# Gated sigmoid over a 256 MB matrix: loads and stores moved from two hardware DMA queues to one software queue, with the one-packet option

## Chip, cores, metric

One core of a Trainium2 chip. The metric is the device time of one execution in microseconds (us); smaller is better. Runs of the kernel before on a single core agree within about 0.2%.

## The reference

```python
def setup_inputs():
    return {"x": np.random.randn(8192, 8192).astype(np.float32)}

def reference(x):
    a, b = np.split(x, 2, axis=-1)
    return a * (1 / (1 + np.exp(-b)))
```

268.4 MB are read and 134.2 MB written: 402.65 MB go through the DMA engines, and per element there are one sigmoid and one multiplication.

## The kernel before

32 tiles of 256 rows. A partition holds two whole rows (64 KB) of x and two rows (32 KB) of the result; there are two slots of each, 192 KB per partition in all. Loads are issued by SyncE, stores by ScalarE, each on its own hardware queue. ScalarE takes the sigmoid in place, VectorE multiplies into the output slot.

```python
R = 2; SLOTS = 2
xs = [pool.tile([P, R * n_cols], fp32, name=f"x_sb{k}") for k in range(SLOTS)]
os = [pool.tile([P, R * half], fp32, name=f"o_sb{k}") for k in range(SLOTS)]
for i in range(n_tiles):
    # ... cut: which slot, which earlier instructions are known to be over
    load = nc.sync.dma_start(out=xs[i % SLOTS], in_=x_t[i])
    # ... cut: the first and last tile are computed in four parts, the others in one
    for k, (r, c) in enumerate(parts):
        b = rows[:, r, 1, c]
        sig = nc.scalar.activation(out=b, in_=b, func=SIG)
        mul = nc.vector.tensor_mul(out=packed[:, r, c], in0=rows[:, r, 0, c], in1=b)
        # ... cut: waits declared as implied; odd sigmoids wait for the old store
    # ... cut: the stores (nc.scalar.dma_start); the last tile's in four pieces
```

Of the kernel before, what the change touches and what calls it, by code (L numbers as in the profile page):

```python
# [1 line left out]

# [4 lines left out]


def _tiles(ctx, tc, x, out):









    nc = tc.nc
    P = nc.NUM_PARTITIONS  # L20
    DEP = mybir.DependencyInfo(mybir.DependencyClass.Sync, mybir.DependencyReason.DATA)
    fp32 = mybir.dt.float32
    SIG = mybir.ActivationFunctionType.Sigmoid

    n_rows, n_cols = x.shape
    half = n_cols // 2
    R = 2
    SLOTS = 2
    n_tiles = n_rows // (P * R)
    x_t = x.rearrange("(n p r) m -> n p (r m)", p=P, r=R)  # L30
    out_t = out.rearrange("(n p r) m -> n p (r m)", p=P, r=R)

    pool = ctx.enter_context(tc.tile_pool(name="io", bufs=1))
    xs = [pool.tile([P, R * n_cols], fp32, name=f"x_sb{k}") for k in range(SLOTS)]
    os = [pool.tile([P, R * half], fp32, name=f"o_sb{k}") for k in range(SLOTS)]

    def implied(later, *earlier):
        for e in earlier:
            tc.declare_no_dep(later.ins, e.ins, reason="follows from the waits that are kept")

    gone = [{k: [] for k in ("loads", "sigs", "muls", "stores")} for _ in range(SLOTS)]
    last_stores = [[] for _ in range(SLOTS)]
    for i in range(n_tiles):
        old = gone[i % SLOTS]
        freed = last_stores[i % SLOTS]
        now = {k: [] for k in old}
        rows = xs[i % SLOTS].rearrange("p (r h m) -> p r h m", r=R, h=2)
        packed = os[i % SLOTS].rearrange("p (r m) -> p r m", r=R)

        load = nc.sync.dma_start(out=xs[i % SLOTS], in_=x_t[i])  # L50
        implied(load, *old["loads"], *old["sigs"])
        now["loads"].append(load)

        if 0 < i < n_tiles - 1:
            parts = [(slice(0, R), slice(0, half))]
        else:
            w = half // 2
            parts = [
                (slice(r, r + 1), slice(c * w, (c + 1) * w)) for r in range(R) for c in range(2)
            ]  # L60
        def store(cols):
            ins = nc.scalar.dma_start(out=out_t[i, :, cols], in_=os[i % SLOTS][:, cols])  # L62
            now["stores"].append(ins)

        chunks = []
# [3 lines that stand above are left out]
            mul = nc.vector.tensor_mul(out=packed[:, r, c], in0=rows[:, r, 0, c], in1=b)  # L69
            implied(sig, *old["sigs"], *old["muls"], *old["loads"])  # L70
            implied(mul, *old["muls"], *old["loads"], *now["loads"])
            by_sigmoid = i % 2 == 1 and len(parts) == 1
            implied(mul, *(s for s in old["stores"] if by_sigmoid or s not in freed))
            if by_sigmoid:
                for s in freed:
                    tc.add_manual_dep(sig.ins, s.ins.name, DEP, reason="frees the output slot")
            tc.keep_in_program_order(sig)
            now["sigs"].append(sig)
            now["muls"].append(mul)
            chunks.append(slice(r.start * half + c.start, r.start * half + c.stop))  # L80
            if i == n_tiles - 1 and k > 0:
                store(chunks[k - 1])
        store(chunks[-1] if i == n_tiles - 1 else slice(0, R * half))
        for s in now["stores"]:
            implied(s, *old["loads"], *old["sigs"], *old["muls"], *now["loads"], *now["sigs"])
        for k in old:
            old[k] += now[k]
        last_stores[i % SLOTS] = now["stores"]


def _launch_early(nc):



    SP = mybir.EngineType.SP
    entry, body = (b.instructions for b in nc.main_func.blocks[:2])
    load = next(i for i in body if i.engine == SP and i.opcode == "DMACopy")
    assert not load.sync_info.on_wait
    body.remove(load)
    where = next(k for k, i in enumerate(entry) if i.engine == SP and i.opcode == "Drain")  # L100
    entry.insert(where, load)


def _close_on_sync(nc):





    SP, POOL = mybir.EngineType.SP, mybir.EngineType.Pool  # L110
    ACT = mybir.EngineType.Activation
    block = nc.main_func.blocks[2].instructions
    waits = block[0]
    assert waits.engine == SP and waits.opcode == "Drain" and len(waits.sync_info.on_wait) > 1
    pool = [i for i in block if i.engine == POOL]
    drain1, gather1, release1, reset, clear, drain2, gather2, release2 = pool
    assert reset.is_reset_sema and clear.opcode == "ISA"
    others = [i for i in block[1:] if i.engine != POOL]
    arrive = [i for i in others[: len(others) // 2] if i.opcode == "Drain"]
    assert len(arrive) == 4  # L120
    body = nc.main_func.blocks[1].instructions
    last = [i for i in body if i.engine == ACT and i.opcode == "DMACopy"][-1].sync_info.on_update[0].id
    final = [w for w in waits.sync_info.on_wait if w.id == last]
    assert len(final) == 1

    def event(engine, wait, update=()):
        return mybir.InstEventSemaphore(
            name=nc.get_next_instruction_name(),
            engine=engine,
            debug=waits.debug,  # L130
            sync_info=mybir.SyncInfo(on_wait=[wait], on_update=list(update)),
        )

    n = len(block)
    for lo, hi in ((reset.reset_range_start, last), (last + 1, reset.reset_range_stop)):
        if lo < hi:
            nc.gpsimd.sem_clear(range(lo, hi))
    clears = block[n:]
    assert clears and all(i.opcode == "ISA" for i in clears)
    back = mybir.SyncUpdate(  # L140
        sync_type="semaphore",
        id=last,
        ant_name=final[0].ant_name,
        update_mode="sem-sub-imm",
        update_value=final[0].wait_value,
        update_reg=None,
    )
    block[:] = [
        *arrive,
        drain1,  # L150
        gather1,
        *(event(POOL, w) for w in waits.sync_info.on_wait if w.id != last),
        reset,
        *clears,
        drain2,
        event(SP, final[0], [back]),
    ]


@with_exitstack  # L160
def kernel(
    ctx: ExitStack,
    tc: tile.TileContext,
    x: bass.AP,
    out: bass.AP,
):
    nc = tc.nc
    with ExitStack() as pools:
        _tiles(pools, tc, x, out)
    tc.close()  # L170
    tc.compile()
    _launch_early(nc)
    _close_on_sync(nc)


# [1 line left out]
_INS = ['x']  # L177
_OUTS = [((8192, 4096), 'float32')]


# [23 lines left out]
```

## Time and profile before

| | before |
|---|---|
| time, median | 933.24 us (933.08 to 933.77, 4 runs) |
| profiled span | 931.7 us |
| VectorE, ScalarE, GpSimd busy | 30%, 24%, 0% |
| DMA engines busy, rate | 9 or 10 tenths in all 40 slices, 432 GB/s |
| a load descriptor (64 KB), a store descriptor (32 KB), on one engine | 2.418 us, 1.213 us |
| one tile on one engine | 29.00 us |

The prediction below shows the page's main lines. Two more pieces are needed for the comparison. The first is the chain of waits of the kernel before in order of time (start, length, what): each piece "DMA" is a load from its issue to its landing, the sigmoid behind it starts when the load has landed, 0.02 to 0.09 us after the last engine's semaphore update.

```profile
60.58 42.21 DMA x_sb<-in_x_dram
...
102.88 7.04 ACT x_sb L68
...
118.66 42.09 DMA x_sb<-in_x_dram
...
160.84 7.04 ACT x_sb L68
...
218.77 7.04 ACT x_sb L68
...
856.90 7.04 ACT x_sb L68
```

The chain walks over every second tile. 102.88, 160.84, 218.77: steps of 57.9 to 58.0 us, two tiles of 29.00. From 102.88 to 856.90 are 754.0 us, 13 steps of 58.00. Nothing is lost from one end to the other.

The second is how the 16 DMA engines run together. A transfer is split over all 16 DMA engines, and each engine posts a short semaphore record (9 ns, 4 bytes) after its share. The time from the first engine's record to the last engine's record of the same transfer I call the **spread**. In the kernel before it is 0.57 us for load 0, 0.61 us for load 10 and 0.65 us for load 31: the engines stay together. A load has landed when the last engine is through. Loads and stores share an engine record by record: of 8238 pairs of successive records on one engine (60 to 890 us of the span, assigned to engines by their times) 8236 go from one queue to the other.

### The profile page before, as it was taken

What the parts mean: (1) busy time and instruction counts of PE and PEld (TensorE: products, weight loads), DVE (VectorE), ACT (ScalarE), POOL (GpSimd) and SP (SyncE); (2) the same over time, 40 slices, a digit from 0 to 9 for tenths busy, and PEclk for the clock granted to TensorE, in tenths of its full rate; (3) what the DMA queues carried; (4) which work ended last, traced back from release to release, by engine and by line L of the source; (5) the groups of instructions that cost most, each with busy time, mean ns of one, the idle gap of its engine ahead of it and who ended that gap; (6) DMA issues with size and microseconds to landing.
All of it is one profiled execution on the core that took longest, in us unless ns stands there. A gap on an engine that the chain in (4) does not pass through costs nothing.

```text
span 931.7 us, 247 instructions
## 1 busy us (share of the span) xinstructions
DVE 278.7 (30%) x38; ACT 227.1 (24%) x39; POOL 0.2 (0%) x4
## 2 busy tenths in 40 slices
DVE  0333213333133331233312333123331233312333
ACT  1323330233311333113331133311333113332033
POOL 0000000000000000000000000000000000000000
DMA  9999999999999999999999999999999999999999
GB/s 405 428 450 428 422 456 405 450 428 428 450 418 438 428 436 442 428 428 450 447 408 428 442 459 428 413 460 411 450 428 425 453 408 447 428 428 450 425 430 405
DMA packets 9649, 402.67 MB, mean 432 GB/s; under 512 B 1072, under 2 KB 1072, under 8 KB 1072
## 3 DMA queue, kind: packets, MB, share of 16 engines
q1 hardware_dynamic: 4608, 268.44, 66.6%
q10 hardware_dynamic: 5040, 134.22, 33.4%
q14 instruction: 1, 0.01, 0.0%
HBM read 268.44 MB, written 134.22 MB: 432 GB/s over the span
## 4 chain that ended last, share of the span: by engine, by line
DMA 73%; DVE 15%; ACT 12%; issue 0%; ACTq 0%
DMA x_sb<-in_x_dram 73%; DVE o_sb L69 15%; ACT x_sb L68 12%; ACTq L62 0%; ACTq L68 0%
## 5 line engine op out<-in xcount | busy, mean ns | idle before, releaser
L69 DVE TENSOR_TENSOR o_sb<-x_sb 128x8192 f32<-128x8192 f32 (+1 forms) x38 | 278.7, 7344 | 647.1 <-ACT x_sb L68 647.1
L68 ACT ACTIVATE x_sb<-x_sb 128x8192 f32<-128x8192 f32 (+1 forms) x38 | 225.8, 5952 | 695.6 <-DMA x_sb<-in_x_dram 694.4
L68 ACT ACT_TABLE_LOAD x1 | 1.3, 1283 | 0.8 <-PEq L188 0.8
L188 POOL MEMSET const-bfloat16-1.0<- 128x1 bf16 x1 | 0.1, 102 | 0.0
L188 POOL MEMSET const-uint8-127<- 128x1 uint8 x1 | 0.1, 102 | 0.0
L188 POOL MEMSET const-float32-0.0<- 128x1 f32 x1 | 0.1, 99 | 0.2 <-issue 0.2
L188 POOL MEMSET const-float32-1.0<- 128x1 f32 x1 | 0.1, 99 | 0.0
## 6 DMA issues: line engine op xcount, KB each, us to landing
out_dram<-o_sb ACTq DMA_DIRECT2D x31, 4096.0 KB, 34.7
out_dram<-o_sb ACTq DMA_DIRECT2D x4, 1024.0 KB, 5.6
x_sb<-in_x_dram SPq DMA_DIRECT2D x32, 42.2
```

Of the source, the lines that this page charges most:

```text
L68: sig = nc.scalar.activation(out=b, in_=b, func=SIG)
L69: mul = nc.vector.tensor_mul(out=packed[:, r, c], in0=rows[:, r, 0, c], in1=b)
L188: nc = _bacc.Bacc("TRN2", target_bir_lowering=False, num_devices=1)
```

## The change

The intent: one queue in which the transfers come in the order in which they are needed, so that a load does not share the engines with a store; fewer waits; and, with the option `single_packet=True`, less time per descriptor. From tile 2 on, store i and load i+2 are issued by GpSimd, right behind each other. Loads 0 and 1 and the four stores of the last tile stay on the hardware queues.

```diff
+    def in_one_packet(out, in_):
+        return nc.gpsimd.dma_start(out=out, in_=in_, single_packet=True)
...
+    def load(i, queue):
+        old = gone[i % SLOTS]
+        ins = queue(out=xs[i % SLOTS], in_=x_t[i])
+        implied(ins, *old["loads"], *old["sigs"])
+        loads.append(ins)
+
+    for i in range(SLOTS):
+        load(i, nc.sync.dma_start)
...
-        load = nc.sync.dma_start(out=xs[i % SLOTS], in_=x_t[i])
-        implied(load, *old["loads"], *old["sigs"])
-        now["loads"].append(load)
...
-            by_sigmoid = i % 2 == 1 and len(parts) == 1
-            implied(mul, *(s for s in old["stores"] if by_sigmoid or s not in freed))
-            if by_sigmoid:
-                for s in freed:
-                    tc.add_manual_dep(sig.ins, s.ins.name, DEP, reason="frees the output slot")
+            implied(mul, *(s for s in old["stores"] if s not in freed))
...
-        store(chunks[-1] if i == n_tiles - 1 else slice(0, R * half))
+        if i == n_tiles - 1:
+            store(chunks[-1], nc.scalar.dma_start)
+        else:
+            store(slice(0, R * half), in_one_packet)
...
+        if i + SLOTS < n_tiles:
+            load(i + SLOTS, in_one_packet)
```

More of the change, by code (lines that the diff above doesn't have):

```diff
@@ L39, in implied @@
             tc.declare_no_dep(later.ins, e.ins, reason="follows from the waits that are kept")
+    def in_one_packet(out, in_):
+        return nc.gpsimd.dma_start(out=out, in_=in_, single_packet=True)
     gone = [{k: [] for k in ("loads", "sigs", "muls", "stores")} for _ in range(SLOTS)]
     last_stores = [[] for _ in range(SLOTS)]
+    loads = []
+    def load(i, queue):
[5 more added lines that the diff above has]
+        load(i, nc.sync.dma_start)
     for i in range(n_tiles):
@@ L46, in _tiles @@
         now = {k: [] for k in old}
+        now["loads"].append(loads[i])
         rows = xs[i % SLOTS].rearrange("p (r h m) -> p r h m", r=R, h=2)
         packed = os[i % SLOTS].rearrange("p (r m) -> p r m", r=R)
-        load = nc.sync.dma_start(out=xs[i % SLOTS], in_=x_t[i])
-        implied(load, *old["loads"], *old["sigs"])
-        now["loads"].append(load)
         if 0 < i < n_tiles - 1:
@@ L60, in _tiles, with store @@
             ]
-        def store(cols):
-            ins = nc.scalar.dma_start(out=out_t[i, :, cols], in_=os[i % SLOTS][:, cols])
+        def store(cols, queue):
+            ins = queue(out=out_t[i, :, cols], in_=os[i % SLOTS][:, cols])
             now["stores"].append(ins)
@@ L81, in _tiles @@
             if i == n_tiles - 1 and k > 0:
-                store(chunks[k - 1])
-        store(chunks[-1] if i == n_tiles - 1 else slice(0, R * half))
+                store(chunks[k - 1], nc.scalar.dma_start)
+        if i == n_tiles - 1:
+            store(chunks[-1], nc.scalar.dma_start)
+        else:
+            store(slice(0, R * half), in_one_packet)
         for s in now["stores"]:
```

## The prediction

> **What bounds the kernel now.** I read the page first: busy shares of the compute engines, then the row of the DMA engines in the 40 slices, then the DMA queues.
>
> ```profile
> DVE 278.7 (30%) x38; ACT 227.1 (24%) x39; POOL 0.2 (0%) x4
> ...
> DMA  9999999999999999999999999999999999999999
> ...
> DMA packets 9649, 402.67 MB, mean 432 GB/s; under 512 B 1072, under 2 KB 1072, under 8 KB 1072
> ...
> q1 hardware_dynamic: 4608, 268.44, 66.6%
> q10 hardware_dynamic: 5040, 134.22, 33.4%
> ```
>
> VectorE and ScalarE are idle for 70% and more; the 16 DMA engines are full in every slice. The two queues (q1 the loads, q10 the stores; columns: packets, MB, share of the 16 engines' span) take 66.6 + 33.4 = 100.0% of the span. There is no hole to fill: the time is the sum of the descriptors' durations. The chain of waits and the queue's own waits look otherwise, and must not mislead:
>
> ```profile
> DMA 73%; DVE 15%; ACT 12%; issue 0%; ACTq 0%
> ...
> SPq L50 <- DVE o_sb L69: 859.9, 30, 31.7
> ```
>
> The chain goes load, sigmoid, multiply, next load, because a load is issued when the multiply has freed its slot. But that load then queues behind the load before it, so the 7.03 + 8.69 us of compute lie beside transfers. This is seen in the timeline of the first tiles (start, duration, engine, operation):
>
> ```profile
> 21.95 7.31 ACT L68 ACTIVATE x_sb<-x_sb 128x2048 f32<-128x2048 f32 x4 [19.89 <-DMA x_sb<-in_x_dram]
> 23.89 8.90 DVE L69 TENSOR_TENSOR o_sb<-x_sb 128x2048 f32<-128x2048 f32 x4 [23.89 <-ACT x_sb L68]
> 32.82 0.38 ACTq L62 DMA_DIRECT2D out_dram<-o_sb  x1
> 44.80 7.03 ACT L68 ACTIVATE x_sb<-x_sb 128x8192 f32<-128x8192 f32 x1 [15.53 <-DMA x_sb<-in_x_dram]
> 51.86 8.69 DVE L69 TENSOR_TENSOR o_sb<-x_sb 128x8192 f32<-128x8192 f32 x1 [19.07 <-ACT x_sb L68]
> 60.58 0.36 ACTq L62 DMA_DIRECT2D out_dram<-o_sb  x1
> 73.65 7.03 ACT L68 ACTIVATE x_sb<-x_sb 128x8192 f32<-128x8192 f32 x1 [21.83 <-DMA x_sb<-in_x_dram]
> ```
>
> Load 1 landed at 44.8, load 2 at 73.65: 28.9 us apart. The store of tile 1 went out at 60.58, and load 3 with it, 13.1 us before load 2 had landed. That is the slack.
>
> The trace's records of single descriptors give the rest. A load has 8 descriptors of 64 KB on each engine (2.418 us each), a store 8 of 32 KB (1.213 us), and one short record of 9 ns for the semaphore. One engine moves one at a time, load, store, load, store, with no gap: from 45 to 930 us of the records they cover 100.2% of the engines' time (neighbours overlap by some ns). From one store's semaphore to the next, one engine needs 29.00 us (65.71, 94.71, 123.71). A tile is 8.389 + 4.194 = 12.583 MB, so the steady rate is 12.583 MB / 29.00 us = 433.9 GB/s.
>
> [...]in the trace load and store descriptors alternate one to one[...].
>
> **The change, part by part.**
>
> Removed: 30 load issues of SP, 31 store issues of ScalarE (0.34 to 0.38 us each, on queues that wait most of the time), and the waits of odd sigmoids on an old store; the multiplies take those waits over. None is on the path that sets the end: minus 0 us.
>
> Moved: 61 transfers onto one queue, in the order store i, load i+2. The bytes are the same, 402.65 MB. In the steady state the queue is strictly first in, first out: store i-1 (9.65 us), load i+1 (19.28 us), store i and so on. Load i lands at time t; store i-1 and load i+1 were queued already at about t - 13.2 (multiply i-1 ends 15.7 us after load i-1 landed, and loads land 28.9 apart: 28.9 - 15.7 = 13.2). They run from t to t + 28.9. Store i is issued at t + 7.03 + 8.69 = t + 15.7, so again with 13.2 us in hand. A dearer issue on GpSimd, even several us[...] fits in there. Steady state: 0 us.
>
> Store slots: multiply i needs store i-2 gone. In the order of the queue that store went out before load i, so it is over 19 us earlier. 0 us.
>
> One packet: [...] I take 2.3 us.
>
> The end: load 31 lands, then store 30 (9.65 us), beside which the four parts of the last tile are computed, then four stores of 1 MB on ScalarE's queue (2.453 us each in the trace now). Before it is the same work in another order, without a hole either. 0 us.
>
> Sum: 933.3 - 2.3 = 931.0 us.
>
> **The rivals.**
>
> (a) A hole at the start[...]. When store 0 is issued (32.82), load 1 is under way on the other queue. In the trace its seventh descriptor starts on one engine at 36.05, store 0's first at 39.14, load 1's eighth at 40.34, and its semaphore comes after a further store descriptor, at 43.97. With store 0 as one packet this turns into: store 0 whole, 39.1 to 48.8; load 1's last descriptor, to 51.2; then the packet of load 2, already queued, 19.3 us, to 70.5; and only then load 1's semaphore. Sigmoid 1 starts at 70.5 rather than 44.8, its multiply ends at 86.3, and store 1 and load 3 cannot be issued before. The queue has nothing from 70.5 to about 88 (86.3[...]): one hole of 17 to 18 us. 931.0 + 17.5 = 948.5 us, 1.6% slower. For it: [...]the mechanism needs only that a one-packet transfer is uninterruptible. Against it: if GpSimd needs over about 3.2 us (36.05 - 32.82) from issue to queue, store 0 comes one turn later, only load 1's semaphore is left, it fires after store 0's packet at about 50.4, and store 1 is ready at 50.4 + 15.7 = 66.1, a few us before load 2 ends at 69.7: no hole. The same if packets are not exclusive. I give the hole three chances in ten.
>
> (b) A bubble between transfers on one queue: 61 of them, each with a semaphore that waits for its data. Against it: where one queue is alone now, there is none. Load 1's first descriptor starts at 21.55 where load 0's semaphore does, and the last stores follow each other every 2.453 us with 8 x 0.309 us in them. For it: the software queue is not in this trace. At 0.5 us each it would be 61 x 0.5 = 30 us, 962 us. One chance in twelve[...].
>
> (c) A gain over 2% would need 914.6 us, 402.65 MB / 914.6 = 440 GB/s even with no start and end[...]. Chance 0.01.
>
> (d) Nothing at all[...]. 933 us.
>
> **Range and chances.** 931.0 is the mode; without the saving 933.3, with all of it and a slightly earlier start 928. The hole of (a) puts a second heap at 946 to 950. A range of 8 in 10 must hold both: 928.0 to 950.0. Two per cent slower is 951.9: only (b) or a larger hole than (a) reaches it, 0.09. Faster by two per cent 0.01. Within, 0.90.
>
> **What would show it.** Right: the DMA row full in all 40 slices, GpSimd's queue with about 95% of the engines' time,[...] landing times of loads near 32 us (13 queued and 19 moving), and the second sigmoid before 51 us. The hole: the second sigmoid starts at about 70, slice 3 or 4 (23.3 us each) falls to a few tenths, and the periods afterwards are whole. A period over 29.0, or a DMA row with eights in it, shows (b). Wrong altogether: descriptors of another size on the software queue, or longer than 2.42 and 1.21 us.

The forecast's sum came to 931.0 us: 933.3 us less 2.3 us for the option. The 9.65 us for a store and 19.28 us for a load are a little short of what the trace before shows, 8 x 1.213 = 9.70 and 8 x 2.418 = 19.34 us, with neighbours overlapping by 3 to 4 ns. In rival (a) it is an assumption, shown nowhere, that a transfer with the option can't be interrupted; and of the hole's 17 to 18 us only 86.3 - 70.5 = 15.8 us come from the trace's times. In rival (c), 440 GB/s stands against the 433.9 GB/s of the trace.

## The result

The changed kernel takes 938.39 us (937.45 to 938.62, 4 runs) against 933.24 us: the ratio is 1.0052, with a 95% interval of 1.0038 to 1.0066, so 0.5% slower. (A ratio here is the mean time of one kernel's fast runs over that of the other's fast runs of the same rounds, so not quite the ratio of the medians quoted.) The page of the changed kernel:

```profile
span 937.3 us, 234 instructions
...
DVE 278.7 (30%) x38; ACT 227.0 (24%) x39; POOL 32.8 (4%) x65
...
DMA  9999999999999999999999999999999999999997
...
q0 software_dynamic: 8784, 381.69, 94.2%
q1 hardware_dynamic: 288, 16.78, 4.3%
q10 hardware_dynamic: 576, 4.19, 1.1%
...
x_sb<-in_x_dram POOLq DMA_DIRECT2D x30, 41.6
```

The work of VectorE and ScalarE is the same. GpSimd now issues 61 transfers at about 0.54 us each. The DMA row is full to the last slice, which has a 7. So the page alone says "still full", and the loss of 5 us isn't in it. It shows in the chain of waits of the changed kernel in order of time:

```profile
44.52 7.04 ACT x_sb L79
...
100.60 7.04 ACT x_sb L79
...
159.67 7.04 ACT x_sb L79
...
218.54 7.04 ACT x_sb L79
...
277.18 7.04 ACT x_sb L79
...
685.59 7.04 ACT x_sb L79
...
743.59 7.04 ACT x_sb L79
...
801.60 7.04 ACT x_sb L79
...
859.85 7.04 ACT x_sb L79
```

The steps are 59.07, 58.87 and 58.64 us at the start and 58.00, 58.01 and 58.25 us near the end. From 100.60 to 859.85 are 759.25 us, against 13 x 58.00 = 754.0: 5.2 us are lost, nearly all before 650 us, a few tenths at each tile.

The records of single descriptors say where. In the next table a column is one load of the changed kernel, by the time at which its first engine is through; below stands how much later the 12th, 13th and 16th engine to finish are (taken from the semaphore records; times from the start of the profiled span, as in the chain above):

```
load through, first engine (us)   70.1   128.2   186.2   244.2   360.2   476.2   592.2   766.2   882.2
12th engine later by              0.34    0.54    0.61    0.61    0.61    0.61    0.61    0.64    0.64
13th engine later by              0.38    0.68    0.96    1.57    3.11    3.95    4.57    4.57    4.57
16th engine later by (spread)     0.64    1.45    2.77    3.35    4.49    5.27    6.04    6.04    6.16
```

Twelve engines keep together and need 29.00 us per tile, just as before. Four fall behind, until the last of them is 6 us late; from about 600 us on it stays so. Since a load has landed only when the slowest engine is through (the next sigmoid starts 0.02 us later), and since the end is the slowest engine's end (its last semaphore update comes at 937.22 us), the kernel pays for the spread: 6.16 - 0.65 = 5.5 us, and the spans differ by 937.26 - 931.72 = 5.5 us.

What the four lose, they lose in single records. A load descriptor lasts 2.418 us. After 45 us of the span, 79 of 3840 load descriptors last over 30 ns longer (up to 0.77 us longer, 22.7 us together); in the kernel before, one of 3840 does. Of the 79, 76 are the **last** descriptor of a load, followed by its semaphore and then a store. No store descriptor is stretched by more than 30 ns. At the ends of loads near 97 and 126 us, 15 and 10 engines are stretched; from about 155 us on it is nearly always the four that are late already.

### The profile page after: what moved, and what is told of

Same layout as the page of the kernel before. It is cut to its first block, busy times and chain, and to the rows that moved or that the text cites. A ratio compares the mean times of both kernels' runs of the same rounds, so it can differ in the third digit from the quotient of the medians.

```text
span 937.3 us, 234 instructions
## 1 busy us (share of the span) xinstructions
DVE 278.7 (30%) x38; ACT 227.0 (24%) x39; POOL 32.8 (4%) x65
## 3 DMA queue, kind: packets, MB, share of 16 engines
q0 software_dynamic: 8784, 381.69, 94.2%
## 4 chain that ended last, share of the span: by engine, by line
DMA 71%; DVE 14%; ACT 12%; POOL 1%; issue 1%; DVEq 0%; ACTq 0%
DMA x_sb<-in_x_dram 71%; DVE o_sb L80 14%; ACT x_sb L79 12%; POOL out_dram L42 1%; DVEq L183 0%; ACTq L73 0%
## 5 line engine op out<-in xcount | busy, mean ns | idle before, releaser
L42 POOL DMA_DIRECT2D out_dram<-o_sb x31 | 16.6, 536 | 872.4 <-DVE o_sb L80 872.4
L42 POOL DMA_DIRECT2D x_sb<-in_x_dram x30 | 16.3, 542 | 0.0
## 6 DMA issues: line engine op xcount, KB each, us to landing
out_dram<-o_sb POOLq DMA_DIRECT2D x31, 4096.0 KB, 22.7
x_sb<-in_x_dram POOLq DMA_DIRECT2D x30, 41.6
```

The source lines that it names most:

```text
L42: return nc.gpsimd.dma_start(out=out, in_=in_, single_packet=True)
```

## The experiments

Three theories came out of the result. **F**: the order. On one queue, first in, first out, all engines end a load together and begin a store together, and this turn costs the engines that are late. **S**: the software queue does it. **P**: the option does it.

Kernels are compared only within the same rounds. The diffs are against the changed kernel.

### The option, the queue, the order

Run 1, without the option:

```diff
-        return nc.gpsimd.dma_start(out=out, in_=in_, single_packet=True)
+        return nc.gpsimd.dma_start(out=out, in_=in_)
```

> The changed kernel without the one-packet option, nothing else. Theory F (the loss comes from first in, first out order on one queue: all engines end a load together and start a store together, and some engines stretch the last load descriptor): 937 to 939 us, spread between the first and last engine's semaphore of a load growing to 5 to 7 us. Theory P (the option itself does it[...]): back to 933 us, spread 0.6 us. Either way the tile period of the undisturbed engines stays 29.00 us.

Measured: 938.27 us, ratio to before 1.0044 (1.0031 to 1.0058); spread growing to 6.22 us, 29.00 us per tile for the first engine, 82 stretched load descriptors. Here five engines end 4.2 to 6.2 us behind the first, not four. Theory P falls: without the option time, tile period and spread are the same.

Run 2, the same order on a hardware queue:

```diff
-        return nc.gpsimd.dma_start(out=out, in_=in_, single_packet=True)
+        return nc.sync.dma_start(out=out, in_=in_)
```

> The same order (store i, load i+2) on one queue, but on SyncE's hardware queue. Theory F (order): 937 to 939 us, stretched last load descriptors of 2.6 to 3.2 us in some engines, spread growing to 5 to 7 us. Theory S (software queue[...]): 932.5 to 933.8 us, spread 0.6 to 0.7 us throughout, no stretched descriptors.

Measured: 938.01 us, 1.0047 (1.0034 to 1.0059); spread growing to 4.83 us, 110 stretched descriptors, 103 of them the last of a load before a store. The lag is shared by more engines: near the end six are 3.2 to 4.8 us behind the first and four more 1.0 to 2.0 us. Without GpSimd and its software queue the loss is the same. The page of this run, engines, DMA row and queues:

```profile
span 936.6 us, 235 instructions
...
DVE 278.7 (30%) x38; ACT 227.0 (24%) x39; POOL 0.2 (0%) x4
...
DMA  9999999999999999999999999999999999999998
...
q1 hardware_dynamic: 9072, 398.46, 98.7%
q10 hardware_dynamic: 576, 4.19, 1.1%
```

Here 98.7% of the engines' time is on SyncE's hardware queue, POOL does nothing. Theory S falls; F predicted it, with a spread a little under its range.

Run 3, only the loads on GpSimd's queue, the stores on ScalarE's:

```diff
-            store(slice(0, R * half), in_one_packet)
+            store(slice(0, R * half), nc.scalar.dma_start)
```

> Loads from tile 2 on on GpSimd's queue with the option, stores on ScalarE's hardware queue as before: two queues, so the engines alternate. Theory F: 933 to 934 us, no growing spread. Theory S: part or all of the loss stays, 935 to 939 us, with stretched load descriptors.

Measured: 933.56 us, 0.9999 (0.9987 to 1.0012); spread 0.62 us, 0.99 at the end; 2 stretched load descriptors.

Run 4, only the stores on GpSimd's queue, the loads on SyncE's:

```diff
-            load(i + SLOTS, in_one_packet)
+            load(i + SLOTS, nc.sync.dma_start)
```

> Stores on GpSimd's queue with the option, loads on SyncE's hardware queue as before: two queues, alternating. Theory F: 933 to 934 us, no growing spread. Theory S: 934 to 937 us[...], otherwise 933 us.

Measured: 934.04 us, 1.0003 (0.9991 to 1.0016); spread 0.42 us, 1.05 at the end; 5 stretched load descriptors. The page of run 3:

```profile
DMA  9999999999999999999999999999999999999999
...
q0 software_dynamic: 4320, 251.66, 62.3%
q10 hardware_dynamic: 5040, 134.22, 33.4%
q1 hardware_dynamic: 288, 16.78, 4.3%
```

With 62.3% of the engines' time on the software queue, and the option on all of it, the last slice is full again. So the four runs agree: the software queue and the option cost nothing and gain nothing, loads and stores on **one** queue cost 0.5%, on **two** they don't. On two queues an engine alternates, record by record (8236 of 8238 pairs in the kernel before), so there the turn is not one of a whole load to a whole store; on the changed kernel's one queue an engine's descriptors come in blocks of 8 loads and 8 stores.

### What the turn needs

Next question: is it the semaphore behind the load that holds an engine (theory M), or the turn from reading HBM to writing it (theory R)?

Run 5, wrong result: stores replaced by loads.

```diff
-            ins = queue(out=out_t[i, :, cols], in_=os[i % SLOTS][:, cols])
+            if i == n_tiles - 1:
+                ins = queue(out=out_t[i, :, cols], in_=os[i % SLOTS][:, cols])
+            else:
+                ins = queue(out=os[i % SLOTS][:, cols], in_=x_t[i, :, cols])
```

> Wrong result on purpose: every store but the last tile's is replaced by a load of the same 4 MB into the same output slot, same queue and order. Theory R (the engines turn from reading HBM to writing it, all at once): no stretched descriptors, spread of a load's semaphores stays under 0.8 us, time 931 to 934 us. Theory M (the semaphore record straight behind a load's last descriptor, with another transfer behind it, holds the engine): spread grows to 5 to 7 us and the time is 937 to 939 us.

Measured: 934.99 us; the spread is 0.5 us over 36 transfers and reaches 1.49 us at the last, by a few single events. 78 load descriptors are stretched, but by 0.09 us on average, and none of them is the last of a load. The descriptors as such are a little longer (2.422 us, 29.06 us per tile); 31 x 0.06 = 2 us cover the 1.4 us over the kernel before (933.62 us in this call). So the time is 1 us above R's range, and R's "no stretched descriptors" and "under 0.8 us" were missed too; M's 937 to 939 us and 5 to 7 us were missed by more. As many semaphores, as many seams, no growth like that of the changed kernel: a semaphore behind a load is not enough, so M as put falls.

Run 6, wrong result: stores replaced by copies from x to out, HBM to HBM.

```diff
-            ins = queue(out=out_t[i, :, cols], in_=os[i % SLOTS][:, cols])
+            src = os[i % SLOTS][:, cols] if i == n_tiles - 1 else x_t[i, :, cols]
+            ins = queue(out=out_t[i, :, cols], in_=src)
```

(Cut: three more lines, which keep its place behind the multiplication and in the order of the queue.)

> Wrong result on purpose: every store but the last tile's is replaced by a copy of 4 MB from x to out, HBM to HBM, issued at the same place. If writing HBM is what disturbs the last load descriptors: stretched last descriptors and a spread growing to several us, as in the changed kernel. If it is the reading of SBUF by the stores: spread stays under 0.8 us. No firm number for the time, a copy within HBM may run at another rate; 931 to 945 us.

Measured: 992.9 us, 1.065, far above the range. The copies themselves take 1.40 us per 32 KB instead of 1.21, and stretched descriptors are everywhere, in the middle of loads too (642 of 3840). The spread reaches 6.9 us, but this traffic is another one, and the run tells nothing on the turn. Inconclusive.

Run 7, each load in two halves behind each other:

```diff
-        ins = queue(out=xs[i % SLOTS], in_=x_t[i])
+        cuts = [slice(0, R * n_cols)] if i < SLOTS else [slice(r * n_cols, (r + 1) * n_cols) for r in range(R)]
+        halves = [queue(out=xs[i % SLOTS][:, c], in_=x_t[i, :, c]) for c in cuts]
...
```

> The changed kernel with each load from tile 2 on cut into two loads of 4 MB, one behind the other: a load's end is followed by a load once and by a store once. Theory R: stretched descriptors only before a store, none at the seam between the two loads, spread 5 to 7 us, time 939 to 941 us[...]. Theory M: stretched descriptors at both places, spread larger, over 942 us.

Measured: 938.57 us, 1.0052 (1.0037 to 1.0067). After the first 55 us, 110 descriptors are stretched: 82 are the last before a store, 1 is at the seam between the two loads, 27 lie elsewhere. So R against M again. But R's figures were off: the spread stopped at 3.7 us, not at 5 to 7, the time is just under its 939 to 941, and the first engine needs 29.07 to 29.09 us per tile. The sum fits: 31 x 0.075 = 2.3 us for the descriptors and 3.5 - 0.6 = 2.9 us of spread, together 5.2; measured 938.57 - 933.62 = 4.95 us.

Run 8, store and load in halves, alternating in the queue:

```diff
...
-            store(slice(0, R * half), in_one_packet)
+            for r in range(R):
+                store(slice(r * half, (r + 1) * half), in_one_packet)
+                tc.keep_in_program_order(now["stores"][-1])
+                if r == 0 and i + SLOTS < n_tiles:
+                    load(i + SLOTS, in_one_packet, 0)
...
-            load(i + SLOTS, in_one_packet)
+            load(i + SLOTS, in_one_packet, 1)
```

(Cut: `load` takes a third argument, 0 for the first half of the load and 1 for the second.)

> The changed kernel with store and load cut in halves and queued store half, load half, store half, load half: twice as many turns from load to store. If each turn costs and goes on costing: spread 10 to 13 us, 945 to 948 us. If the loss is bounded (it stops once the late engines are some 5 us apart from the others): spread 5 to 7 us, 940 to 943 us[...].

Measured: 938.70 us, 1.0054 (1.0039 to 1.0069); spread 2.9 us at 134 us of the span and 3.3 us from some 230 us to the last tiles; 29.09 us per tile for the first engine. Twice as many turns did not cost twice as much: the loss is bounded, and the engines stop losing once they are far enough apart. It was below both ranges; by the same sum, 31 x 0.087 = 2.7 us plus 3.3 - 0.6 = 2.7 us make 5.4, measured 5.1.

Run 9, half of each store on ScalarE's queue:

```diff
-            store(slice(0, R * half), in_one_packet)
+            store(slice(0, half), in_one_packet)
+            store(slice(half, R * half), nc.scalar.dma_start)
```

> The changed kernel with half of each store (2 MB) on ScalarE's hardware queue, the other half and the load first in, first out on GpSimd's queue. The half on ScalarE's queue mixes with the load that is running when it is issued, so stores flow already when that load ends, but a block of pure store follows it. Theory P (the cost is that stores begin after a pause of some 19 us in which there are none, while late engines still read): spread under 1 us, 934.5 to 936 us[...]. Theory B (the cost is the late engine's last reads beside a pure block of stores of the engines ahead): spread grows to 3 to 6 us, 937 to 940 us.

Measured: 939.02 us, 1.006 (1.0043 to 1.0077); the spread of the transfers on GpSimd's queue grows to between 3.3 and 4.6 us; 251 load descriptors are stretched, by order of start 171 of them the last and 63 the seventh of a load's eight. So it isn't enough that stores flow already when a load ends: theory P (here the pause, not the option) falls. B (a pure block of stores behind the load) fits; the run that was to test it from the other side is run 10, and it failed.

Run 10, half of each load on SyncE's queue:

```diff
-        ins = queue(out=xs[i % SLOTS], in_=x_t[i])
+        n = 1 if i < SLOTS else 2
+        w = R * n_cols // n
+        cuts = [slice(k * w, (k + 1) * w) for k in range(n)]
+        queues = [queue] if i < SLOTS else [in_one_packet, nc.sync.dma_start]
+        pieces = [q(out=xs[i % SLOTS][:, c], in_=x_t[i, :, c]) for c, q in zip(cuts, queues)]
...
```

> The changed kernel with half of each load (4 MB, descriptors of 32 KB) on SyncE's hardware queue, store and other half first in, first out on GpSimd's. The store is then mixed with half a load, and a block of pure load of some 10 us remains. Theory P: the pause without stores is about 10 us, spread grows, to 2 us or more, 937 to 939 us. Theory B: there is no pure block of stores, spread under 1 us, 934.5 to 936 us (8 more descriptors per tile).

Measured: 960.88 us, 1.029. This one failed as a test. The half on SyncE's queue overtook the other queue's half of the load before (median 24.3 us from issue to landing against 43.6), so two tiles landed close together and then a long wait followed: sigmoids start at 309.2, 350.4, 369.7 and 410.7 us, 41, 19 and 41 us apart. The waits:

```profile
ACT x_sb L84 <- DMA x_sb<-in_x_dram: 722.4, 32, 36.5
DVE o_sb L85 <- ACT x_sb L84: 661.4, 33, 33.4
```

ScalarE's longest wait for a load is 36.5 us, against 22.7 us in the changed kernel, and one engine's records have a gap of 1.2 us at every second tile (305.6 to 306.8 us, 366.3 to 367.5 us) with stretched loads behind it. The order of landing was changed, not only the mix; nothing follows on P and B.

Run 11, each load in four (descriptors of 16 KB):

```diff
-        ins = queue(out=xs[i % SLOTS], in_=x_t[i])
+        n = 1 if i < SLOTS else 4
+        w = R * n_cols // n
+        cuts = [slice(k * w, (k + 1) * w) for k in range(n)]
+        queues = [queue] if i < SLOTS else [in_one_packet] * 4
+        pieces = [q(out=xs[i % SLOTS][:, c], in_=x_t[i, :, c]) for c, q in zip(cuts, queues)]
...
```

> The changed kernel with each load from tile 2 on cut into four of 2 MB one behind the other, so descriptors of 16 KB instead of 64 KB. In the runs so far the spread stopped growing at 5 to 6 us with descriptors of 64 KB and at 3.3 to 3.6 us with 32 KB. If the bound goes with the load descriptor's time: spread 1.5 to 2.2 us. If it is a fixed time: 3.3 us or more. Time 938 to 940 us[...].

Measured: 942.14 us, 1.0093 (1.0078 to 1.0108); spread 3.2 us. That is just under the range for a fixed time and well above the other. So the bound does not go in proportion to the descriptor's time: it is 4.8 to 6.2 us with 64 KB, 3.3 to 3.7 with 32 KB and 3.2 with 16 KB. (71 load descriptors are stretched, 52 of them among the last three of a load's 32.) The time was above the range because a further descriptor cost more than I had reckoned with: the first engine needs 29.21 us per tile, 212 ns more for 24 more data descriptors and 3 more semaphores, 7.9 ns each (run 7: 75 ns for 9, 8.3 each; run 8: 87 ns for 18, 4.8 each). 31 x 0.212 = 6.6 us and 3.2 - 0.6 = 2.6 us make 9.2; measured 9.0.

Run 12, wrong result: stores replaced by copies within SBUF.

```diff
-            ins = queue(out=out_t[i, :, cols], in_=os[i % SLOTS][:, cols])
+            if i == n_tiles - 1:
+                ins = queue(out=out_t[i, :, cols], in_=os[i % SLOTS][:, cols])
+            else:
+                ins = queue(out=os[i % SLOTS][:, half:], in_=os[i % SLOTS][:, :half])
```

> Wrong result on purpose: every store but the last tile's is replaced by a copy of 2 MB within SBUF (one half of the output slot onto its other half), same place, same queue: SBUF is still read by it, but nothing is written to HBM. If the loads are stretched by the writing of HBM: no growth, spread under 1 us. If it is the reading of SBUF that begins when a load ends: spread grows to 3 us or more. The time says little, since 2 MB less are moved per tile: with tiles of 24.2 us, some 32 x 24.2 us and the ends, about 785 us.

Measured: 787.18 us (2 MB less per tile), 24.24 us per tile; the spread is 0.50 us over 38 transfers, then 1.06 us, 1.27 us at the end, by two single events; 2 stretched load descriptors. The copies read SBUF and stand in the queue where the stores did, with half the bytes; and blocks of store as short as these, with the same time per block, did let the spread grow in run 8. So writing HBM is part of it, reading SBUF is not enough.

### Taken together

| order of transfers | runs | spread, start to end (us) | stretched load descriptors |
|---|---|---|---|
| loads and stores on two queues | before, 3, 4 | 0.4 to 0.65, up to 1.05 | 1 to 5 |
| load, store on one queue | changed, 1, 2 | 0.6 to 4.8 to 6.2 | 79 to 110 |
| the same, loads or both in smaller pieces | 7, 8, 11 | 0.5 to 3.2 to 3.7 | 71 to 141 |
| one queue, no HBM write | 5, 12 | 0.5 to 1.3 to 1.5 | 78 (5, of some 90 ns), 2 |

(Run 9, with half of each store on a second queue, belongs to the second row: 3.3 to 4.6 us, 251 descriptors, 0.6% slower. So a second queue alone does not avoid the loss; in the runs without it the second queue carried all loads or all stores. Runs 6 and 10 are left out as inconclusive.)

Shown: the loss comes with blocks of load and of store behind each other on one queue, and not with the software queue or the option; taking the writes to HBM away, in two ways, took the growth away (runs 5 and 12); it is a stretch at the end of loads, mostly of their last descriptor, on engines that are late, and it ends when they are 3 to 6 us behind. Not shown: why the last read of a late engine lasts longer, why only some engines stay behind (four in the changed kernel, five in run 1, six by over 3 us in run 2), which ones (the records do not name them), and what sets the bound.

The traces rule out one easy reading, that any read is slowed by the writes of other engines. In the changed kernel some 340 load descriptors end while at least eight engines are writing. Of those with a semaphore record right behind them (within 12 ns), the last of their load, 65 of 233 are stretched, of the others 1 of 104. In the kernel before 1680 load descriptors end so, and 1 is stretched. So being beside writes is not enough; the place at the end of a load, with a block of stores behind it, counts too. Whether it is the engine's own turn to the stores or the block of stores of the engines ahead, no run separates. No run looked into the HBM.

No version here beats the kernel before. Runs 3 and 4 are the same as it within 0.2%.

## Why the prediction was right or wrong

The measured 938.39 us lie in the range of 928 to 950 us, and "within 2%" was given 0.90. But the range was that wide for a reason that did not happen, and the sum behind 931.0 failed in two of its terms, so that the time fell into the range by luck: the cost that was met stands nowhere in the prediction.

- **Bound, waits, slack: right.** The DMA engines stay full (9 tenths or more in 39 of 40 slices), the compute stays beside the transfers. GpSimd's issues of 0.54 us and its 32.7 us of waiting at most cost nothing; runs 3 and 4 show it separately.
- **"One packet": minus 2.3 us, wrong.** The saving was my estimate, and no trace had shown it. The first engine needs 29.00 us per tile with the option (changed kernel) and without (run 1). The term is 0. (With the option the page still counts 8784 packets on GpSimd's queue, 61 x 16 x 9: each descriptor and each semaphore record by itself.)
- **"Steady state: 0 us", the term that was missing.** The order came as told (on each engine 8 store descriptors, then 8 load descriptors, 9.68 and 19.32 us with their semaphore record where nothing is stretched), but the working treated the 16 engines as one. Each of them turns from load to store by itself, the load lands with the last, and four drift off, the slowest by 5.5 us. That covers the difference: 933.3 - 0 + 5.5 = 938.8 against 938.39.
- **Rival (a), the hole at the start: did not happen.** GpSimd's store 0 went out at 33.12 us, its first descriptor started at 38.77 us on the engine looked at, load 1's last at 39.98 us, and load 1's semaphore came at 43.61 us: the same alternation as before (39.14, 40.34, 43.97), one descriptor each, so a store with the option did not hold the engine to its end, as the rival had assumed. The second sigmoid started at 44.52 us. The top of the range stood on this rival. (Of the delay to the first byte in its hole the trace before shows one case: load 0's first descriptor starts 1.0 us after its issue.)
- **Rival (b), a bubble between transfers: wrong as put, near in kind.** There is no bubble at a semaphore, neither behind loads nor behind stores: in the changed kernel a next record starts within 4 ns of the end of each of 912 semaphore records (60 to 890 us). There is a loss behind loads, and the evidence that I took against it, load 0 followed by load 1 and store by store, has no turn from load to store in it. It would have taken a look at such a turn on one queue, and the trace before has none.
- **"The end: 0 us."** The engines that are ahead wait at the end: twelve are through with store 30 by 921.5 us, and the last tile's stores start at 923.0 us. That is part of the 7 in the last slice. It adds nothing, as the late engines set the end.
- **The signs.** The full row, 94.2% on GpSimd's queue and the second sigmoid before 51 us came as told; a period under 29.00 us did not. The landing time of loads was put at 32 us and is 41.6 us (42.2 before): the store that lies between in the queue (9.7 us) had been left out of that sum.

## What to carry to other kernels

Here the page showed the DMA engines full on both sides and hid a drift between the 16 of them, a spread of 0.65 us before and 6.16 us after: compare when the first and the last engine finish the same transfer. A queue that kept "the right order" was not free here. Two queues, one with the loads and one with the stores, kept the engines together (933.56 and 934.04 us in runs 3 and 4); one queue with whole loads and whole stores in turn cost 0.5%, whether GpSimd or SyncE issued it (938.39 us in the changed kernel, 938.01 us in run 2).
